# A hybrid attention and SSD layer: sums of squares and split operands made in the SSD stage, output weights asked for throughout the last pair

## The chip, the cores and the metric

The kernel runs on one core of one Trainium2 chip. The metric is the device time of one execution in microseconds. The engines are named as in the profile: PE (TensorE, matmuls), PEld (its weight loads), DVE (VectorE), ACT (ScalarE), POOL (GpSimd) and SP (SyncE, which here only issues DMAs). Sixteen DMA engines serve the core. DMAs are issued from SP's queue or from POOL's.

## The reference, cut to what matters

A decoder layer with two branches. The sequence has 2048 positions, the model 1024 columns. The attention branch has 16 heads in three dilations (1, 4 and 16), combined by their log-sum-exps; the SSD branch is a chunked scan over 16 chunks of 128 positions. Each branch is gated, normed by its root mean square, and multiplied with its half of the output weights.

```python
y_att = rms_norm(y_att.reshape(Bsz, S, D_ATT) * jax.nn.silu(z_att), att_norm_g[layer])
...
y = ssd_chunked(xs_h, dt, a, bm, cm)
y = y + d_skip[layer].astype(jnp.float32)[:, None] * xs_h
y_ssm = rms_norm(y.reshape(Bsz, S, D_SSM).astype(x.dtype) * jax.nn.silu(z_ssm), ssm_norm_g[layer])

mix = jnp.concatenate([y_att, y_ssm], axis=-1)
out = jnp.einsum('bse,ed->bsd', mix, w_out[layer])
x = layer_norm(alpha * x + out, ln_g[layer], ln_b[layer])
```

with `rms_norm(u, g) = u * rsqrt(mean(u * u) + 1e-5) * g`. The gain g is folded into the output weights, so the kernel multiplies the gated rows as they are and scales each product by the row's own rsqrt afterwards. For that it needs two things of every gated block: its split into a high and a low part for the matmuls, and the sum of its squares along the columns.

## The kernel before, in words

All large matmuls are made in three parts: each operand x is split into hi (x rounded to the matmul's format) and lo = x - hi, and hi*hi, hi*lo and lo*hi are accumulated.

The first half of the kernel works through input projections (`proj`, 24 matmuls for each block of 512 positions, lines 104 to 114). Its last part is the SSD stage: while 20 projections of queries, keys and gates run on PE, the 32 units of the scan, `ssd(n, g)` for chunk n and group g, are fed in between (lines 340 to 432), 32 units over 20 projections. A scheduler orders the instructions of this half from its own estimates of their durations. A unit ends with `y`, the gated output, 128 columns-in-group by 4 blocks by 128 positions, in fp32 (DVE adds at line 400, POOL multiplies with the gate at line 401). Line 402 stores y to the DRAM tensor `d_us`. For n under 4 it also splits y into yh (ACT) and yl (DVE) and stores both to `d_uh` (lines 412 to 418). The tiles of yh and yl are those of the unit's `xdeh` and `xdel`, one buffer each.

The second half is the attention, in eight pairs of heads, each with three dilations d, four quarters qd and two halves: 24 steps a pair. Order on PE, DVE, ACT and POOL is written out by hand (`manual_schedule`); only SP's queue is ordered by the scheduler. A step issues `scores` for itself, `transposes` for the step two before and `values` for the step three before; `at` in the loop is the (d, qd, half) of the `values` step. ACT copies finished numerators into tiles `num`. After a pair, its statistics go out to DRAM (`statistics`, d_st), come back in another layout (`gather`, cm), become weights (`weights`), go out (d_wd) and come back broadcast over partitions (wb), and `combine(A, d)` multiplies and adds the three dilations. For pairs 0 to 6 that happens during the next pair, on POOL, at four places of its loop (`step`), and the gated result is stored in `d_ua`. For pair 7 nothing of the attention is left to run beside it: `weights` and `combine` of pair 7 stand in the output stage, on DVE, and its result stays in SBUF (`u7`).

The output stage makes 32 products: `product(n, br)` for a block n of 128 positions and a branch br (1 is SSD, 0 is attention), 48 matmuls of 128x128 by 128x512 in two halves of 24, each over the eight row blocks e of the branch's weights, W[8*br + e]. The order is (0,1), (1,1), (2,1), (3,1), then (0,0) to (3,0), then (4,1), (4,0), (5,1), (5,0) and so on. A product (n, 0) needs the result of pair 7; the first four do not. Around it, for each product: `fetch_parts` takes a large tile for the split operand (for br = 1 and n under 4 it is loaded from d_uh), `fetch_raw` loads the unsplit rows (d_us or d_ua), `split` makes hi and lo on ACT and DVE, `squares` squares them on ACT and sums them on DVE into `sr`, and between the halves of the product one small matmul with a column of ones (line 743) sums that over the partitions. `add` takes the root, and adds the scaled product to the residual in `O[n]`; `norm` ends the block.

The output weights `d_wo` are 16 loads of 1 MB (`load_w`) into tiles that the attention has used: 8 to 15 (SSD) during pair 7 into old key, query, v and permuted-query tiles, 0 to 7 after `combine(A, 2)` in the second turn of the output loop, the first four into `num` tiles. All are issued from POOL's queue, behind whatever POOL has to do.

These lines give the rings that the tiles come from, with their number of buffers:

```python
ring = {"qh": (io, 1), "ql": (io, 1), "qp": (io, 4), "v": (io, 3), "num": (cm_, 6), "wb": (cm_, 3)}
ring.update({f"k{p}_{i}": (qk[i], 1) for p in "hl" for i in range(2)})
```

Of the kernel before, what the change touches and what calls it, by code (L numbers as in the profile page):

```python
# [9 lines left out]
F32 = mybir.dt.float32  # L10
F32R = mybir.dt.float32r
# [17 lines left out]
def hybrid_layer(ctx, tc, xT, xc, w52, wv, convw, convb, dtb, alog, dskp, gcol, wout,  # L29
# [26 lines left out]
    d_us = [dtile(f"d_us{g}", [16, 128, 4, 128]) for g in range(2)]  # L56
    d_uh = [dtile(f"d_uh{g}", [4, 128, 2, 4, 128]) for g in range(2)]
# [10 lines left out]
    gc = consts.tile([128, 16], F32, name="gc")  # L68
    def evac(i, o, a):
        if i % 2:  # L70
            nc.vector.tensor_copy(o, a)
        else:
            nc.scalar.copy(o, a)


    with ExitStack() as c1:
# [263 lines left out]
        def ssd(n, g):  # L340
# [61 lines left out]
            nc.sync.dma_start(d_us[g][n], y)  # L402
# [9 lines left out]
            if n < 4:  # L412
                yh, yl = [sd.tile([128, 512], F32R, name=f"xde{p}") for p in "hl"]
                y1 = y.rearrange("p c l -> p (c l)")
                nc.scalar.copy(yh, y1)
                nc.vector.tensor_tensor(yl, y1, yh.bitcast(F32), op=OP.subtract)
                for p, t in enumerate((yh, yl)):
                    nc.sync.dma_start(d_uh[g][n][:, p], v4(t.bitcast(F32)))
# [20 lines left out]
    with ExitStack() as c2:  # L439
# [244 lines left out]
        def fetch_parts(n, br):  # L684

            t = SP[n, br] = free.pop(0) if len(free) else big(UT.pop(0))
            if br and n < 4:
# [3 lines left out]

        def fetch_raw(n, br):
            u = raw[n, br] = row().rearrange("p (c t) -> p c t", t=128)
            if br:
                for g in range(2):
                    (nc.gpsimd if n < 2 else nc.sync).dma_start(u[:, 4 * g:4 * g + 4], d_us[g][n])
            else:
                nc.sync.dma_start(u[:, 0:7], d_ua[n])

        def split(n, br, cs=slice(0, 8)):  # L700

            if br and n < 4:
                return
            u, t = raw[n, br], SP[n, br]
            if not br and cs.stop == 8:
                nc.vector.tensor_copy(u[:, 7, :], u7[n // 4][:, n % 4])
# [3 lines left out]
        def squares(n, br):  # L710
            u = raw.pop((n, br))
            nc.scalar.activation(u, u, AF.Square)
            sr[n, br] = f2(io.tile([128, 2, 256], F32, name="tb1", bufs=1))[:, 0:128]
            nc.vector.tensor_reduce(sr[n, br], u.rearrange("p c t -> p t c"), axis=mybir.AxisListType.X, op=OP.add)  # L714
# [6 lines left out]
        raw, sr = {}, {}  # L721
# [3 lines left out]
        def product(n, br):  # L725
# [4 lines left out]
            for hf in range(2):  # L730
# [10 lines left out]
                if hf == 0:  # L741
                    pn = psN.tile([128, 512], F32, name="N")
                    nc.tensor.matmul(pn[:, 0:1], sr.pop((n, br)), one, start=True, stop=True)  # L743
            free.append(t)
            return pss, pn

        def add(n, br, pss, pn):

            r = small[:, 8 * n + br:8 * n + br + 1]
            nc.scalar.activation(r, pn[:, 0:1], AF.Sqrt, bias=epst, scale=1.0 / D)  # L750
            nc.vector.reciprocal(r, r)
# [28 lines left out]
        def gate(d, eng):  # L780
            num = f2(pairs[7]["num"][d])
            eng.tensor_tensor(num, num, zt7, op=OP.mult)
# [7 lines left out]
        with tc.manual_schedule(engines={E.PE, E.DVE, E.Activation, E.Pool}):  # L790
            for i in range(len(todo) + TA + 1):
# [16 lines left out]
                if i > TA:  # L808
# [10 lines left out]
                    step = ((1, 0, 0), (1, 1, 0), (1, 3, 0), (2, 2, 0))  # L819
                    if pr and at in step:  # L820
# [141 lines left out]
```

## Time and profile before

| | before |
|---|---|
| median of 3 runs | 2193.69 us (2192.73 to 2193.98) |
| the profiled execution's own time | 2193.83 us |
| its span, first to last instruction | 2192.0 us |
| mean granted PE clock | 0.984 |
| PE busy, share of the span | 98% |
| DVE, ACT, POOL busy | 53%, 39%, 38% |
| DMA, mean | 166 GB/s |

Input projections run until about 700 us of the span, the SSD stage from 700 to about 1262, the attention until about 1780, the handover and the output products to the end. A busy PE is not PE at its peak, since matmuls are pipelined; the useful reading is where it is idle, and what ended the idle time. In the timeline and the chain, a row has start, length, engine, line and output<-input. In the waits, a row has the waiting engine and line, the releaser, and after the colon the total, the number of times and the longest, in microseconds.

### The profile page before, as it was taken

Reading aid. Unit: us, or ns where it says so; the run is one execution under the profiler, and the core shown is the slowest. Engines: PE = TensorE matmul, PEld = TensorE weight load, DVE = VectorE, ACT = ScalarE, POOL = GpSimd, SP = SyncE. Lnnn points to the kernel's source line nnn. Section 1 sums busy time; section 2 is a strip of 40 time slices with the busy share of each in tenths; the row PEclk is TensorE's granted clock in tenths of the full one; section 3 lists DMA queues with packets and bytes.
Section 4 is the critical chain, followed back from the end, with each engine's and each line's share of the span. In section 5 each row is a group of like instructions: output and inputs, shape, how many; then the busy total and the mean of one; then the engine's idle time right before and its main releaser. Section 6 shows DMA issues by size and latency. Waiting matters only on the chain.

```text
span 2192.0 us, 37071 instructions
## 1 busy us (share of the span) xinstructions
PE 2138.5 (98%) x13968; PEld 1784.6 (81%) x13968; DVE 1166.2 (53%) x2941; ACT 847.8 (39%) x2289; POOL 838.8 (38%) x589
## 2 busy tenths in 40 slices
PE   8999999999999999999999999999999976999998
PEld 8999888888888888888888878888878865888886
DVE  4000255555223555554544258888888845655655
ACT  4101122223112333232345368887888841222221
POOL 3101010102442455555555321776666670322322
PEclk9999999999999999999999979999999988999999
DMA  8644222224786656555543542777876799232220
GB/s 281 182 133 139 70 78 71 77 71 148 249 262 208 206 194 198 178 190 177 171 157 129 195 148 76 228 219 223 241 216 184 208 360 276 99 104 83 93 84 29
DMA packets 213955, 363.66 MB, mean 166 GB/s; under 512 B 37776, under 2 KB 125968, under 8 KB 203536
## 3 DMA queue, kind: packets, MB, share of 16 engines
q1 hardware_dynamic: 197408, 278.45, 41.8%
q0 software_dynamic: 16368, 82.84, 10.6%
q8 instruction: 110, 1.80, 0.3%
q14 instruction: 69, 0.57, 0.1%
HBM read 226.62 MB, written 134.61 MB: 165 GB/s over the span
## 4 chain that ended last, share of the span: by engine, by line
PE 89%; DMA 4%; DVE 4%; ACT 2%; SPq 1%; issue 1%; POOL 0%; DVEq 0%; POOLq 0%; ACTq 0%
PE pp L112 14%; PE pp L111 14%; PE pp L113 14%; PE N L577 6%; PE T L557 6%; PE S L528 6%; PE S L737 3%; PE S L739 3%; PE S L738 3%; PE pp L155 2%; PE pp L156 2%; PE pp L154 2%; PE T L737 2%; PE T L738 2%; PE T L739 2%; PE ss L386 1%
## 5 line engine op out<-in xcount | busy, mean ns | idle before, releaser
L111 PE MATMUL pp<-xh,whi 128*128 128x512 f32 x1408 | 550.3, 391 | 0.0
L112 PE MATMUL pp<-xl,whi 128*128 128x512 f32 x1408 | 549.6, 390 | 0.0
L113 PE MATMUL pp<-xh,wlo 128*128 128x512 f32 x1408 | 548.5, 390 | 0.0
L544 ACT ACTIVATE P<-P,st 128x256 f32<-128x256 f32 (+1 forms) x768 | 345.4, 452 | 94.7 <-DVE st L536 94.1
L113 PEld LDWEIGHTS pp<-xh,wlo 128*128 128x128 f32 x1408 | 264.3, 188 | 55.4
L111 PEld LDWEIGHTS pp<-xh,whi 128*128 128x128 f32 x1408 | 264.4, 188 | 54.7
L112 PEld LDWEIGHTS pp<-xl,whi 128*128 128x128 f32 x1408 | 264.4, 188 | 54.0
L536 DVE CUSTOM_DVE_ANT_0 P<-S,tb 128x256 f32<-128x256 f32 (+1 forms) x768 | 235.3, 362 | 107.3 <-PE S L528 76.1
L101 POOL TENSOR_TENSOR wlo<-wraw,whi 128x1024 fp32r<-128x1024 f32 x44 | 105.5, 2397 | 365.1 <-ACT whi L100 352.1
L559 DVE COPY PT<-T 128x512 f32<-128x512 f32 (+1 forms) x304 | 196.5, 677 | 2.3 <-PE T L557 2.2
L557 PE MATMUL T<-ident,P 128*128 128x128 f32 x1200 | 179.4, 286 | 6.3 <-DVE PT L559 5.9
L577 PE MATMUL N<-PT,v 128*64 128x128 f32 x2400 | 176.4, 284 | 0.0
L577 PEld LDWEIGHTS N<-PT,v 128*64 128x64 f32 x2400 | 129.2, 138 | 33.2 <-issue 22.6
L557 PEld LDWEIGHTS T<-ident,P 128*128 128x128 f32 x1200 | 129.7, 142 | 31.5 <-DVE PT L559 7.3
L544 ACT ACTIVATION_READ_ACCUMULATOR P<-P,st 128x1 f32 x768 | 144.7, 188 | 0.0
L644 POOL TENSOR_TENSOR wb<-num,wb 128x2048 f32<-128x2048 f32 x21 | 96.3, 4586 | 97.1 <-DMA wb<-d_wd 69.3
L528 PE MATMUL S<-kh,qp 64*128 64x256 f32 (+1 forms) x1024 | 126.3, 306 | 0.0
L379 DVE TENSOR_SCALAR mt<-csb,cs 128x128 f32<-128x128 f32 x256 | 75.2, 363 | 71.2 <-DMA csb<-d_cs 71.2
L714 DVE TENSOR_REDUCE tb<-P 128x128 f32<-128x1024 f32 x32 | 64.0, 2000 | 85.6 <-PE N L743 49.2
L528 PEld LDWEIGHTS S<-kh,qp 64*128 64x128 f32 x1024 | 88.8, 188 | 22.0 <-issue 20.9
L154 PE MATMUL pp<-vh,xh 128*128 128x384 f32 (+1 forms) x304 | 95.0, 320 | 6.0 <-ACT xh L184 5.4
L100 ACT CAST whi<-wraw 128x1024 fp32r<-128x1024 f32 x44 | 46.1, 1047 | 138.3 <-PE pp L112 130.5
(295 smaller groups left out, 3807.1 us busy)
## 6 DMA issues: line engine op xcount, KB each, us to landing
v<-d_v POOLq DMA_DIRECT2D x24, 1024.0 KB, 7.0
wb<-d_wd SPq DMA_DIRECT2D x48, 512.0 KB
wraw<-w SPq DMA_DIRECT2D x44, 512.0 KB
d_wo<-wot SPq DMA_DIRECT2D x32, 512.0 KB
csb<-d_cs SPq DMA_DIRECT2D x32, 512.0 KB
d_v<-vt SPq DMA_DIRECT2D x64, 192.0 KB
d_za<-ev SPq DMA_DIRECT2D x32, 256.0 KB
d_xs<-cvo SPq DMA_DIRECT2D x8, 1024.0 KB
```

The source lines that it names most:

```text
L111: nc.tensor.matmul(ps, hi[:, k, :], h, start=(k == 0), stop=False)
L112: nc.tensor.matmul(ps, hi[:, k, :], l, start=False, stop=False)
L113: nc.tensor.matmul(ps, lo[:, k, :], h, start=False, stop=(k == 7))
L154: nc.tensor.matmul(ps, h, vw[k][0], start=(k == 0), stop=False)
L528: nc.tensor.matmul(ov(sp[h][:, 256 * b:256 * b + w]), A["q"][d][x][hr, blk], kv(A["k"][y][hr]), start=(m == 0), stop=(m == 2))
L536: nc.vector.tensor_tensor_reduce(P[:, h, b, 256 - w:256], sp[h][:, c0:c0 + w], tab[:, h, tab.shape[2] - w:], 1.0, 3.0e38, OP.add, OP.min, ...
L544: nc.scalar.activation(p, p, AF.Exp, bias=stat(A, 0, d, h, blk), scale=-1.0, accum_out=stat(A, 1, d, h, blk))
L557: nc.tensor.transpose(tp[:, h, b], P[:, h, b, 128 * which:128 * which + 128], ident)
L559: nc.vector.tensor_copy(pt[:, :, bl[0]:2], tp[:, :, bl[0]:2])
L577: nc.tensor.matmul(nm[64 * h:64 * h + 64, bq * 128:bq * 128 + 128], v[:, k, 64 * h:64 * h + 64], pts[which][:, h, b], start=(f or not whic ...
L737: nc.tensor.matmul(ps, uh[:, e, :], wh, start=(e == 0), stop=False)
L738: nc.tensor.matmul(ps, uh[:, e, :], wl, start=False, stop=False)
```

## The change

Three parts.

1. In `ssd`, y is no longer stored whole. Every unit now splits y and stores yh and yl in d_uh, which holds all 16 chunks. Every unit also squares y on POOL (into xd), sums over its four blocks on DVE (into cbm), sums over partitions by a matmul with `one` into a new PSUM tile pq, and adds that to column n of a constant tile `ssq` on DVE.
2. In the output stage, SSD operands are loaded finished from d_uh, by POOL's queue. `fetch` stands for `fetch_parts` and `fetch_raw`; `split`, `squares` and the small matmul in `product` are left for br = 0 alone. The roots of all 16 sums are taken at once behind the first product.
3. The requests of the last pair (output weights 8 to 15, pair 7's gate z7, the first two operands) are spread over pair 7 by `last_pair(at)` and one place before it; the first residuals are asked for behind the first product instead of ahead of it.

```diff
@@ ssd @@
             nc.gpsimd.tensor_tensor(y, y, zt, op=OP.mult)
-            nc.sync.dma_start(d_us[g][n], y)
+            nc.gpsimd.tensor_tensor(xd, y, y, op=OP.mult)
+            nc.vector.tensor_reduce(cbm, xd.rearrange("p c l -> p l c"), axis=mybir.AxisListType.X, op=OP.add)
+            pq = ss.tile([128, 512], F32, name="ss")
+            nc.tensor.matmul(pq[:, 0:1], cbm, one, start=True, stop=True)
+            if g:
+                nc.vector.tensor_tensor(ssq[:, n:n + 1], pq[:, 0:1], ssq[:, n:n + 1], op=OP.add)
+            else:
+                nc.vector.tensor_copy(ssq[:, n:n + 1], pq[:, 0:1])
...
-            if n < 4:
-                yh, yl = [sd.tile([128, 512], F32R, name=f"xde{p}") for p in "hl"]
-                ...
+            yh, yl = [sd.tile([128, 512], F32R, name=f"xde{p}") for p in "hl"]
+            y1 = y.rearrange("p c l -> p (c l)")
+            nc.scalar.copy(yh, y1)
+            nc.vector.tensor_tensor(yl, y1, yh.bitcast(F32), op=OP.subtract)
+            for p, t in enumerate((yh, yl)):
+                nc.sync.dma_start(d_uh[g][n][:, p], v4(t.bitcast(F32)))
@@ fetch, product, add @@
+        def fetch(n, br):
             t = SP[n, br] = free.pop(0) if len(free) else big(UT.pop(0))
-            if br and n < 4:
+            if br:
                 for g in range(2):
                     nc.gpsimd.dma_start(t.rearrange("p (a c t) -> p a c t", a=2, t=128)[:, :, 4 * g:4 * g + 4],
                                         d_uh[g][n])
             else:
+                u = raw[n] = row().rearrange("p (c t) -> p c t", t=128)
                 nc.sync.dma_start(u[:, 0:7], d_ua[n])
...
-                if hf == 0:
+                if hf == br == 0:
                     pn = psN.tile([128, 512], F32, name="N")
...
+            r = ssq[:, n:n + 1]
+            if not br:
+                r = small[:, 8 * n:8 * n + 1]
+                nc.scalar.activation(r, pss.pop(1)[:, 0:1], AF.Sqrt, bias=epst, scale=1.0 / D)
+                nc.vector.reciprocal(r, r)
@@ the last pair @@
+        def last_pair(at):
+            if at == (0, 0, 0):
+                load_w(8, "kh_0")
+                load_w(9, "kl_0")
+            elif at == (0, 3, 1):
+                load_w(12, "v")
+            elif at == (1, 0, 0):
+                z7.append(big("num", F32))
+                nc.gpsimd.dma_start(z7[0], d_za[7])
+            elif at == (1, 1, 0):
+                fetch(0, 1)
+            elif at == (1, 3, 0):
+                load_w(13, "qp")
+                load_w(14, "qp")
+                gate(0, nc.gpsimd)
+            elif at == (1, 3, 1):
+                load_w(15, "v")
+                fetch(1, 1)
...
+                    if pr == 7 and at == (0, 3, 0):
+                        load_w(10, "qh")
+                        load_w(11, "ql")
...
-                    elif at == (1, 0, 0):
-                        for e, name in ((8, "kh_0"), (9, "kl_0"), (10, "qh"), (11, "ql"), (12, "v")):
-                            load_w(e, name)
-                    elif at == (1, 1, 0):
-                        zt7 = big("num", F32)
-                        nc.gpsimd.dma_start(zt7, d_za[7])
-                    elif at == (1, 3, 0):
-                        for e, name in ((13, "qp"), (14, "qp")):
-                            load_w(e, name)
-                        fetch_parts(0, 1)
-                        gate(0, nc.gpsimd)
-                    elif at == (1, 3, 1):
-                        load_w(15, "v")
-                    elif at == (2, 2, 0):
-                        fetch_parts(1, 1)
@@ output stage @@
-            fetch_raw(0, 1)
-            squares(0, 1)
-            residual(0)
-            fetch_raw(1, 1)
-            residual(1)
-            fetch_parts(2, 1)
-            fetch_raw(2, 1)
...
                     weights(A, 0)
                     weights(A, 1)
+                    nc.scalar.activation(ssq, ssq, AF.Sqrt, bias=epst, scale=1.0 / D)
+                    nc.vector.reciprocal(ssq, ssq)
+                    residual(0)
+                    residual(1)
+                    fetch(2, 1)
                     gate(1, nc.vector)
                     gate(2, nc.vector)
                 if i == 1:
-                    fetch_parts(3, 1)
-                    fetch_raw(3, 1)
+                    fetch(3, 1)
...
                 if i == 2:
-                    split(0, 0, slice(0, 7))
+                    split(0, slice(0, 7))
+                if i + 1 < len(order) and not order[i + 1][1]:
+                    split(order[i + 1][0], slice(7, 8) if i == 3 else slice(0, 8))
+                    squares(order[i + 1][0])
+                if 2 <= i < len(order) - 2 and order[i + 2][1]:
+                    residual(order[i + 2][0])
```

The weights 0 to 7, the combine of pair 7 and the order of the 32 products are as they were.

More of the change, by code (lines that the diff above doesn't have):

```diff
@@ L55, in hybrid_layer @@
     d_cs = dtile("d_cs", [256, 128])
-    d_us = [dtile(f"d_us{g}", [16, 128, 4, 128]) for g in range(2)]
-    d_uh = [dtile(f"d_uh{g}", [4, 128, 2, 4, 128]) for g in range(2)]
+    d_uh = [dtile(f"d_uh{g}", [16, 128, 2, 4, 128]) for g in range(2)]
     d_wo = dtile("d_wo", [16, 128, 2, D])
```

57 lines of the change are left out of this document (18 added, 39 removed).

## The prediction

> **What bounds the kernel now.** I read, in this order, the page's busy shares, a table of windows by stage, TensorE's waits, and the chain of waits from the end of the attention onward.
>
> ```profile
> PE 2138.5 (98%) x13968; PEld 1784.6 (81%) x13968; DVE 1166.2 (53%) x2941; ACT 847.8 (39%) x2289; POOL 838.8 (38%) x589
> 700.00:1262.00 562.00, 562.00 (x3043) 462.94 (x3042) 273.61 (x524) 194.84 (x283) 291.11 (x212) 1.00 0.54 181
> 1780.00:1785.00 5.00, 0.00 (x0) 0.00 (x0) 0.00 (x0) 0.34 (x2) 4.98 (x3) 0.77 1.12 385
> 1950.00:2100.00 150.00, 150.00 (x663) 122.12 (x662) 87.16 (x107) 37.81 (x53) 38.16 (x14) 1.00 0.26 85
> PE N L743 <- DVE tb L714: 23.7, 2, 19.2
> PE S L737 <- DMA num<-d_uh: 7.0, 1, 7.0
> ```
>
> A window's columns are its length, then PE, PEld, DVE, ACT, POOL busy, granted clock, DMA share, GB/s. TensorE is the bound: full in the SSD stage (700 to 1262) and in the steady output stage (1950 to 2100), so TensorE work added or removed there counts in full, and other engines' work there counts only if TensorE comes to wait for it (DVE is busy 274 us of 562, POOL 291). The one loss of size is where the attention hands over to the output products: 7.0 us for the first operands, 4.5 and 19.2 us for sums of squares. These are the waits that the change removes; the chain shows what would be late next.
>
> ```profile
> 1777.66 1.92 PE N L577 x32
> ...
> 1781.75 11.66 DMA d_st<-sT
> 1793.49 11.46 DMA cm<-d_st
> ...
> 1807.45 3.21 DMA d_wd<-cm
> ...
> 1814.25 24.14 DMA wb<-d_wd
> 1838.49 2.30 DVE wb L644
> ...
> 1841.42 1.89 DVE PT L649 x3
> ...
> 1865.08 0.39 PE L737 MATMUL S<-num 128*128 128x512 f32 x1
> ```
>
> Columns: start, length, what. Attention ends at 1779.6. Statistics go to DRAM, come back, become weights, go out again and come back broadcast (wb); DVE combines the last pair until 1843.3. Meanwhile TensorE has only the four SSD products (0..3,1); the first attention product, (0,0), which needs the combined pair, starts at 1865.08. The 19.2 us wait is product (2,1) whose sum of squares stands on DVE behind the combine. So 1865 is not the chain's limit: one and a half products were left to do when the chain was through.
>
> **The change, part by part.**
>
> *SSD stage, TensorE.* Each of 32 units gains one matmul of a 128-row column of sums with `one`; the 16 SSD products lose theirs. Its slot is seen in a steady product:
>
> ```profile
> 1995.05 0.39 PE L739 MATMUL S<-wb,num 128*128 128x512 f32 x1
> 1995.28 0.28 PE L743 MATMUL N<-one,tb 128*128 128x1 f32 x2
> ...
> 1995.73 0.39 PE L738 MATMUL S<-num 128*128 128x512 f32 x1
> ```
>
> From 1995.05 to 1995.73 is 0.68 us where two 0.23 steps would be 0.46: 0.22 us each (0.14 if it lands beside other small ones). Added 32 x 0.22 = +7.0 us (4.5 at least), all on the path. Removed where TensorE is full, 12 x 0.22 = -2.6; the other four lie inside the idle stretch.
>
> *SSD stage, other engines.* Per unit POOL gains a square, DVE a reduction and a tiny add, and for the 24 units with n from 4 on ACT a cast, DVE a subtraction. SP issues two d_uh stores in place of one d_us store, or of three for n under 4.
>
> ```profile
> L401 POOL TENSOR_TENSOR y<-y,zt x32: 1284/1289/2220, 706.2 to 1239.6; 128x512 f32<-128x512 f32 x32
> L415 ACT CAST xdeh<-y x8: 621/622/627, 707.5 to 831.8; 128x512 fp32r<-128x512 f32 x8
> L416 DVE TENSOR_TENSOR xdel<-y,xdeh x8: 673/679/683, 710.1 to 834.6; 128x512 fp32r<-128x512 f32 x8
> L714 DVE TENSOR_REDUCE tb<-P 128x128 f32<-128x1024 f32 x32 | 64.0, 2000 | 85.6 <-PE N L743 49.2
>   POOL xdel L371: 11.9, 2
> 1240.91 0.75 POOL L462 DMA_DIRECT2D qh<-d_qh  x1
> 1267.05 0.33 PE L528 MATMUL S<-kh,qh 64*128 64x128 f32 x2
> ```
>
> POOL +32 x 1.29 = 41 us, DVE +32 x 1.15 (half the 2.00 reduction, and 0.15 as an estimate for the add) + 24 x 0.68 = 53, ACT 15: POOL 332 of 562, DVE 327, all beside TensorE; I cost it at nothing. The yh and yl tiles are those of xde, so the next unit waits for the stores; the fifth row is that wait after L418, in units that already stored both halves, and TensorE stayed full. If the cover went, the price is whatever the new matmul waits: 0 to 1.3 us per unit (one POOL square late). The queued work behind a waiting matmul would be projections that need nothing. I take 0, since the stage's many matmuls on DVE, ACT and POOL results cost no idle time now; the upper end is a rival below. The last unit's longer tail delays the first attention loads (from 1240.9 on) by perhaps 5 us; the first scores come at 1267.05, after projections that hide it.
>
> *Last pair.* Weights 8 to 11 are asked for by POOL some 20 us earlier, weight 12 some 12, the gate 10 and the first operands 13. POOL stood idle 16.2 us there, waiting for wb:
>
> ```profile
> 1730.19 1.20 POOL L472 DMA_DIRECT2D v<-d_v  x1
> 1747.60 4.57 POOL L644 TENSOR_TENSOR wb<-num,wb 128x2048 f32<-128x2048 f32 x1 [16.21 <-DMA wb<-d_wd]
> 1764.66 4.60 POOL L644 TENSOR_TENSOR wb<-num,wb 128x2048 f32<-128x2048 f32 x1
> 1765.75 0.57 ACT L587 COPY num<-N 128x512 f32<-128x512 f32 x1
> 1769.04 1.09 PE L557 MATMUL T<-ident,P 128*128 128x128 f32 x8
> ```
>
> The issues fit into it. But v of the third dilation now queues behind four weights (needed only by the third dilation's values), and 6 MB share the engines with wb: the combine starts between 1747.6 and 1755; I take 1750. From there POOL has multiply, gate load, multiply, add, two operand issues, multiply: 4.6+0.6+4.6+4.6+1.4+4.6 = 20.4 us to 1770.4. By program order the operands of (1,1) now take the second old num slot and the third dilation's num takes the slot that this last multiply frees, so ACT's copy at 1765.75 would wait 4.7 us; behind it on ACT stand the exponentials. A step's exponentials are about 3.3 us ahead of their transposes (those that end where the copy starts, 1765.75, feed the transposes of 1769.04), so TensorE loses about 1.5 us; ends 0 and 6.4.
>
> *Handover.* The first operands have landed, so (0,1) starts at once; it may stop for weight 15, which POOL asks for no earlier than before, and that costs nothing because the chain is later. The chain: nothing in it is edited, but it shares DMA engines with less. The raw copies (2 MB here) are gone, the weights mostly moved earlier. Quiet prices from earlier pairs:
>
> ```profile
> 1470.83 1.79 SPq L605 DMA_DIRECT2D d_st<-sT  x4
> 1475.81 0.38 SPq L611 DMA_DIRECT2D cm<-d_st  x1
> 1352.73 0.38 SPq L611 DMA_DIRECT2D cm<-d_st  x1
> 1359.20 0.18 DVE L618 TENSOR_TENSOR mm<-cm 128x32 f32<-128x32 f32 x1
> 1370.00:1375.00 5.00, 5.00 (x64) 4.22 (x62) 4.51 (x20) 3.80 (x16) 0.00 (x0) 1.00 1.04 228
> 1390.00:1395.00 5.00, 5.00 (x60) 4.20 (x60) 4.37 (x17) 3.67 (x14) 4.64 (x5) 1.00 1.12 418
> 1810.68 4.16 SPq L642 DMA_DIRECT2D wb<-d_wd  x6
> ```
>
> Statistics out: 11.2 us now (last issue ends 1782.25), 3.2 quiet; I take 7, as weights 13 to 15, operands and residuals still move then. Back in: 11.5 now, at most 6.5 quiet; I take 8.5. The wb loads: 27.8 us from 1810.68 to 1838.5; 3 MB at the 228 GB/s of a wb stretch is 13.8, 15.5 with latency; I take 21, as weights 0 and 1 and a d_ua row (2.5 MB at 418 GB/s, 6 us) stay beside them. Together 4.2+3.0+6.8 = 14.0 us earlier (ends 0 and 25.3), less the 1.5 of the last pair: combine ends at 1830.8.
>
> What is late next is weights 3 to 7, which POOL issues only behind the slot that the last multiply frees:
>
> ```profile
> 1841.29 0.53 POOL L675 DMA_DIRECT2D num<-d_wo  x1 [7.23 <-issue]
> 1843.61 0.54 POOL L675 DMA_DIRECT2D wb<-d_wo  x1 [0.19 <-issue]
> DMA to landing us min/median/max: 15.0/16.4/17.8
> 1845.00:1850.00 5.00, 4.85 (x12) 3.90 (x13) 4.93 (x8) 0.26 (x1) 0.00 (x0) 0.50 1.03 379
> ```
>
> Weight 7 lands 17.8 us after 1843.61, at 1861.4, 18.1 after the combine. Before, that was hidden by the leftover products; now (0,0) waits for it. I take 16.5 (two d_ua rows can come sooner). Then 0.7 for its last three matmuls, 5.5 for the second half (24 x 0.23), and 2.5 because the clock is at 0.50 after idling (12 matmuls in 5 us): (0,0) ends 25.2 after the combine, at 1856.0, against 1865.1 + 11.3 (48 steps and a sum) = 1876.4 before: -20.4. The Trainium skill, "DMA: Bandwidth & Descriptors", section "Anatomy of one DMA — SWDGE (gpsimd) path", gives 2.0 us plus bytes over 436 GB/s; by that, as an estimate, five weights are there 14 us after the first issue, and the sum would be 2173. The trace's 20 us from 1841.3 to 1861.4, with other transfers alongside, disagrees, and the row is used.
>
> *Steady stage.* Operands of later SSD products come as finished halves through POOL, 1 MB for 0.5 MB at 85 GB/s of traffic, behind the norm's POOL work but two products (22 us) ahead: nothing.
>
> **Sum.** +7.0 - 2.6 - 20.4 = -16.0 on the profiled execution's 2193.83 us (span 2192.0): 2177.8, taken as 2178. The median of the runs is 2193.69, 0.14 lower. Differences under 0.2% (4.4 us) can't be told from no change.
>
> **Rivals.**
> - A, the chain is no faster: saturated engines (share 1.12 at 1780) stay saturated by the weights and residuals. Then (0,0) ends 1843.3+1.5+25.2 = 1870.0, -6.4; total 2191.8. Against: fewer bytes there.
> - B, the chain is quiet: 25.3 us earlier, at 1818; TensorE's four products decide (1779.6 + 4 x 11.3 = 1825, some 7 us later if weight 15 stops the first); (0,0) ends near 1843, -33.5; total 2162.2 with the cheap matmul. Against: 8 MB still to move.
> - C, slower: TensorE runs in order and waits for each new sum of squares, at the end of a chain y, gate, square, reduce over two engines. The cost decides from 16.0/32 = 0.50 us per unit; at one late square of 1.29 it is +41, 2219. For it: L401 took up to 2220 ns in place of 1289, and cbm is now held until the matmul has read it. The Trainium skill, "GPSIMD Engine Reference", section "1. Specifications", says that POOL's memory interfaces are shared with VectorE and contend with its two-input instructions; the 2220 agrees. Against: the full TensorE of 700 to 1262.
> - D, the last pair stalls: combine from 1755, 6.4 us; total 2182.7.
>
> **How the numbers follow.** My case 0.47, A 0.14, B 0.15, C 0.12, D 0.12. Faster: mine, B, D and the better edge of A, 0.77; the same: the rest of A, 0.11; slower: C, 0.12. The range leaves out C and the outermost of B: 2163 to 2196, its top being chain unmoved and D's stall at once (-20.4 vanishes: 2198, trimmed).
>
> **What would show it.** Right: about 32 small matmuls in 700 to 1275 with that stage some 7 us longer and TensorE without idle; no wait of 7 us at the attention's end; one TensorE wait before or inside (0,0), for the combine or for weights 4 to 7; (0,0) ending about 20 us closer to the attention's end. Wrong: TensorE waiting for the reduction in the SSD stage (C), ACT idle at its num copies in the last pair (D), statistics and wb as slow as now (A), or the SSD stage reordered in a way that no row here shows.

## The result, and the profile after

The kernel before took 2193.21 us in the runs beside it (median of 4), the changed kernel 2322.56 us (median of 4): a ratio of 1.0595, 95% interval 1.0577 to 1.0614. The profiled execution of the changed kernel has a span of 2319.6 us against 2192.0. Forecast were 2178 us, and 2163 to 2196 as the range.

The page's busy shares of the changed kernel, then a table of windows (length, then PE, PEld, DVE, ACT, POOL busy, granted clock, DMA share, GB/s):

```profile
PE 2170.9 (94%) x14000; PEld 1810.5 (78%) x14000; DVE 1160.6 (50%) x2986; ACT 835.8 (36%) x2272; POOL 868.6 (37%) x641
```

```profile
700.00:1240.00 540.00, 540.00 (x2811) 446.37 (x2811) 248.25 (x474) 185.72 (x266) 237.81 (x178) 1.00 0.47 160
1240.00:1399.00 159.00, 61.51 (x323) 50.62 (x321) 68.78 (x140) 30.70 (x47) 68.42 (x63) 0.58 0.31 106
```

TensorE is as full in the first 540 us of the SSD stage as it was before. Then it is busy for 61.5 of 159 us, at a clock of 0.58. No other engine is near full there. The list of TensorE's waits from 1240 to 1400 says what it waits for (total, times, longest):

```profile
PE ss L406 <- DVE cbm L404: 69.6, 9, 8.6
PE ss L386 <- DVE mt L382: 21.8, 8, 3.9
PE S L535 <- DMA kh<-d_kh: 6.5, 1, 6.5
```

L406 is the new matmul of the sums (in the kernel before, the number is that of the state matmul, which is L414 in the changed kernel). It waits nine times, in the last nine units. Until then it never waits, but its place shows. Here is the timeline of TensorE in the stretch where projections still cover the units, in the kernel before and then in the changed one. Only SSD instructions are shown; what is left out between L396 and L406 of the changed kernel is projections.

```profile
866.01 1.09 PE L386 MATMUL ss<-mt,xdt 128*64 128x128 f32 x16
867.04 1.16 PE L396 MATMUL ss<-bc,H 128*128 128x128 f32 x8
867.95 0.48 PE L406 MATMUL ss<-xdeh,bsh 128*128 128x512 f32 x1
...
868.73 0.60 PE L355 MATMUL ss<-ident,xs 128*128 128x128 f32 x4
```

```profile
872.34 1.09 PE L386 MATMUL ss<-mt,xdt 128*64 128x128 f32 x16
873.36 1.16 PE L396 MATMUL ss<-bc,H 128*128 128x128 f32 x8
...
888.00 0.28 PE L406 MATMUL ss<-one,cbm 128*128 128x1 f32 x2
888.14 0.48 PE L414 MATMUL ss<-xdeh,bsh 128*128 128x512 f32 x1
...
888.92 0.60 PE L355 MATMUL ss<-ident,xs 128*128 128x128 f32 x4
```

Before, a unit's products L386 and L396 are followed at once by its state matmul (xdeh, bsh), and 0.8 us later by the next unit's transposes L355: two units are in flight. After, 13.5 us of projections stand between L396 and the sum, and the state matmul and the next unit's transposes stand behind the sum. Units begin every 23 us in place of every 17, the projections are used up with nine units to go, and these run bare, with nothing else for TensorE to do, one every 18 us:

```profile
1297.38 2.08 PE L396 MATMUL ss<-bc,H 128*128 128x128 f32 x8
1308.04 0.59 PE L406 MATMUL ss<-one,cbm 128*128 128x1 f32 x2 [8.58 <-DVE cbm L404]
...
1309.91 1.06 PE L355 MATMUL ss<-ident,xs 128*128 128x128 f32 x4
```

The table gives three parts of each profiled execution: the start of the first attention score, the attention from there to the end of its last values matmul, and the rest.

| kernel | median us | ratio to before (95%) | first score | attention | rest |
|---|---|---|---|---|---|
| before | 2193.2 | | 1267.1 | 512.7 | 412.2 |
| after | 2322.6 | 1.0577 to 1.0614 | 1399.5 | 531.8 | 388.4 |
| e1_own_targets | 2368.0 | 1.0782 to 1.0818 | 1440.6 | 531.4 | 394.5 |
| e2_deferred_sum | 2270.9 | 1.0345 to 1.0376 | 1344.9 | 529.6 | 394.2 |
| e3_both | 2232.1 | 1.0163 to 1.0197 | 1299.9 | 531.3 | 396.9 |
| e4_no_squares | 2192.3 | 0.9993 to 1.0013 | 1270.0 | 529.5 | 390.1 |
| e5_late_fetch | 2227.3 | 1.0146 to 1.0195 | 1302.9 | 530.8 | 390.2 |
| e6_requests_as_before | 2219.3 | 1.0117 to 1.0150 | 1302.2 | 523.9 | 396.3 |
| e7_square_on_act | 2234.8 | 1.0186 to 1.0226 | 1306.9 | 533.4 | 390.9 |
| e8_first_four_sums | 2199.5 | 1.0024 to 1.0049 | 1276.7 | 528.0 | 393.3 |
| e9_own_slot | 2200.8 | 1.0030 to 1.0060 | 1278.2 | 528.7 | 391.1 |
| e10_old_requests | 2192.3 | 1.0000 to 1.0018 | 1276.7 | 516.0 | 396.4 |
| e11_square_to_xd | 2196.3 | 1.0017 to 1.0037 | 1277.7 | 522.2 | 395.9 |
| e12_own_sum_tile | 2325.6 | 1.0597 to 1.0641 | 1397.8 | 530.8 | 394.0 |
| e13_all_mended | 2203.1 | 1.0045 to 1.0085 | 1277.2 | 523.2 | 400.4 |
| e14_four_sums_spread | 2191.8 | 0.9997 to 1.0018 | 1272.1 | 517.1 | 401.8 |
| e15_four_sums_old | 2184.7 | 0.9965 to 0.9993 | 1269.4 | 515.8 | 395.8 |

The three parts are read from the one profiled execution of each kernel. It lies up to 4.7 us from the median of the kernel's runs, so a sum of parts can miss a difference of medians by a few microseconds.

So the change adds 132.4 us ahead of the attention and 19.1 in it, and takes 23.8 off the rest: 127.7, close to the difference of the spans. Of the 132.4, 97.5 is TensorE idle from 1240 to 1399, some 26 the clock (an estimate: 61.5 us of work at 0.58, times 0.42), and some 7 the new matmuls. Of the 19.1, 6.5 lies in the first pair and 12.1 in the last. The last pair's wait:

```profile
PE T L564 <- ACT P L551: 9.2, 1, 9.2
```

```profile
1899.33 4.59 POOL L651 TENSOR_TENSOR wb<-num,wb 128x2048 f32<-128x2048 f32 x1 [23.08 <-DMA wb<-d_wd]
1904.49 4.58 POOL L651 TENSOR_TENSOR wb<-num,wb 128x2048 f32<-128x2048 f32 x1
1915.12 4.50 POOL L651 TENSOR_TENSOR wb<-num,wb 128x2048 f32<-128x2048 f32 x1
```

```profile
1915.12 4.51 POOL wb L651
...
1919.66 0.58 ACT num L594
1920.24 0.51 ACT P L551 x2
...
1920.79 0.47 PE T L564
```

POOL's three multiplies of pair 6's combine, then the chain of waits: ACT's first copy into the third dilation's num starts 0.03 us after the third multiply ends, and exponentials and transposes stand behind it. The rest is shorter because the chain behind the attention is, at every transfer (start, length, from the chain of waits; then DVE's third multiply of the last combine, from the timeline):

```profile
1933.23 5.43 DMA d_st<-sT
...
1938.81 8.92 DMA cm<-d_st
...
1950.23 2.41 DMA d_wd<-cm
...
1955.74 14.78 DMA wb<-d_wd
...
1980.58 17.64 DMA wb<-d_wo
```

```profile
1975.46 2.29 DVE L651 TENSOR_TENSOR wb<-num,wb 128x2048 f32<-128x2048 f32 x1 [3.65 <-DMA wb<-d_wd]
```

The chain's row for wb ends at 1970.5, where the chain passes to POOL's queue. The last of the wb loads lands later: DVE's third multiply waits for it until 1975.46. The chain's last line is weight 7, of weights 4 to 7, now the last link.

### The profile page after: what moved, and what is told of

Read it like the earlier page. It is cut to its first block, busy times and chain, and to the rows that moved or that the text cites. A ratio compares the mean times of both kernels' runs of the same rounds, so it can differ in the third digit from the quotient of the medians.

```text
span 2319.6 us, 37246 instructions
## 1 busy us (share of the span) xinstructions
PE 2170.9 (94%) x14000; PEld 1810.5 (78%) x14000; DVE 1160.6 (50%) x2986; ACT 835.8 (36%) x2272; POOL 868.6 (37%) x641
## 5 line engine op out<-in xcount | busy, mean ns | idle before, releaser
L564 PEld LDWEIGHTS T<-ident,P 128*128 128x128 f32 x1200 | 131.2, 144 | 40.4 <-ACT P L551 10.7
L155 PE MATMUL pp<-vl,xh 128*128 128x384 f32 (+1 forms) x304 | 96.8, 320 | 0.1
```

What stands on the lines that cost most here:

```text
L155: nc.tensor.matmul(ps, h, vw[k][1], start=False, stop=False)
L564: nc.tensor.transpose(tp[:, h, b], P[:, h, b, 128 * which:128 * which + 128], ident)
```

## The experiments

Times and stages are in the table above. Two causes were suspected in the SSD stage: the place of the sum's PSUM tile in the ring of five (six tiles per unit, granted in the order in which they are written down), and the reuse of xd and cbm as targets.

**Own targets.**

```diff
-nc.gpsimd.tensor_tensor(xd, y, y, op=OP.mult)
-nc.vector.tensor_reduce(cbm, xd...)       # and pq <- cbm
+nc.gpsimd.tensor_tensor(e2, y, y, op=OP.mult)
+nc.vector.tensor_reduce(ones, e2...)      # and pq <- ones
```

> The changed kernel, but the square goes to e2 and the column of sums to the tile of ones (done with by then), so the next unit's xd and cbm wait for neither. The sum's PSUM tile stays where it was, ahead of pst. Theory ring: the ss pool grants its buffers in written order, so pst and the next unit's px can't be placed before the sum's tile is, and that tile waits for y, gate, square and reduction; this is still there, the units still run one after another, some 9 to 11 are left uncovered at about 15 us of idle TensorE each: the SSD stage stays +135 to +170 and the whole 2315 to 2350. Rival targets: the next unit waits for xd and cbm; this is gone, and the whole is 2193 + 7 (32 matmuls at 0.22) + 14 (last pair) - 24 (handover) = 2190. Rival halves: the y halves of all n hold the xde buffers; untouched here, about 2320.

Measured 2368, worse by 45 us than the change. TensorE now waits at the sum eleven times:

```profile
PE ss L406 <- DVE ones L404: 79.3, 11, 7.8
PE ss L386 <- DVE mt L382: 44.3, 10, 5.4
```

That is above the 2315 to 2350 expected by the ring theory, and far from the 2190 of the targets theory. The targets are not the cause where the sum's place in the ring is as in the change. That it got worse is due to e2: e12 below, which differs from this run in the square's tile alone, takes 2325.6. The next unit writes e2 early and xd late.

**The sum in the next unit.** The sum's matmul and its PSUM tile stand behind the next unit's px, ahead of its cbm; targets as in the change.

```diff
+if prev: sumsq(*prev.pop())               # ahead of cbm of the next unit
 cbm = sd.tile([128, 128], F32, name="cbm")
```

> The changed kernel, but the sum's matmul and its PSUM tile stand in the next unit, behind px and ahead of cbm, so no tile of the ring waits for the y chain before px. Square and sum still go to xd and cbm. Theory ring alone: units overlap again, 2190. Theory targets: the next unit's cbm still waits for the sum's matmul, some 5 units are left without projections at 10 to 15 us of idle each: +50 to +75 in the SSD stage, 2235 to 2265. Both at once (each suffices to keep units apart): 2235 to 2265 here and no gain in the run with own targets. Rival halves: about 2320.

Measured 2270.9: a little above the 2235 to 2265 of the two-cause theory. Some 40% of the loss is gone, six units are left bare, and the wait is for cbm's reduction again:

```profile
PE ss L344 <- DVE cbm L418: 40.0, 6, 7.4
```

**Both.** Square to e2, sum to the tile of ones, matmul in the next unit behind pst.

```diff
-(square, reduction, pq, its matmul and add, ahead of pst)
+if prev: sumsq(*prev.pop())               # behind pst: the unit before; pq, matmul, add
+nc.gpsimd.tensor_tensor(e2, y, y, op=OP.mult)      # at the unit's end
+nc.vector.tensor_reduce(ones, e2...)
```

> The changed kernel with both: square to e2, sums to the tile of ones, and the sum's matmul with its PSUM tile in the next unit, behind pst. If ring and targets are the whole cause: SSD stage +7 (32 matmuls at 0.22; at least 4.5), attention +14, handover -24: 2190, between 2185 and 2197. If either alone was the cause, the same. Rival halves (the y halves of all n in the xde buffers, with twice the stores): still above 2250. Rival engines (POOL's square and DVE's reduction overload them): above 2220.

Measured 2232, 42 above what was expected, in the range of the rival engines. Units overlap again, and no unit is bare, but TensorE waits some 16 us in the stage, and the projections from 700 us to the first score take 470 us in place of 462 (from start to next start, idle time left out):

```profile
PE ss L416 <- POOL xdel L381: 5.4, 10, 0.8
PE ss L416 <- ACT xdeh L380: 4.7, 3, 1.7
PE ss L396 <- DVE mt L392: 4.1, 4, 1.8
```

**No squares.**

```diff
-nc.gpsimd.tensor_tensor(xd, y, y, op=OP.mult)   # and reduction, matmul, add
+if not g and not n: nc.vector.memset(ssq, 1024.0)
```

> The changed kernel without the sums of squares: square, reduction, matmul and add are left out and the 16 columns set to a constant, so the output isn't the reference's. The y halves of all n and the last pair's requests stay. Ring or targets: 2183 (the run with both, less 7 of matmuls), SSD stage within 5 us of the kernel before. Rival halves: SSD stage still over 60 us longer, 2250 and up.

This kernel leaves out the sums and sets the columns to a constant. Measured 2192.3, the time of the kernel before and 9 above what was expected. The first score is 3 us late, so the halves for all n and their buffers cost the SSD stage next to nothing: that rival falls. It is the sums that cost 130 us. The rest of the change is no gain either: what the handover wins (22 us) the attention gives back (17).

**The last pair: (1,1) later; the requests put back; the square on ACT.** All three on the run with both.

```diff
 elif at == (1, 3, 1):
     load_w(15, "v")
-    fetch(1, 1)
+elif at == (2, 0, 0):
+    fetch(1, 1)
```

> The run with both mended (e2, ones, deferred sum), and one more edit: the operands of (1,1) are asked for at (2,0,0), behind the third dilation's num tile, in place of (1,3,1), ahead of it. Theory slot: of the six num slots, (1,1) took the one that the second multiply of pair 6's combine freed, so ACT's copy into the third dilation's num waited for the third multiply and the transposes 8 to 9 us behind it. With the order turned round, that copy finds a free slot: the wait at the transposes goes (under 1 us), the last pair is 8 us shorter, and the whole 2232 - 8 = 2224 (2219 to 2228). (1,1)'s operands then land some 10 us later, still ahead of its product. Rival: POOL is late because of the added issues and bytes, whichever tile takes the slot: the wait stays, 2232.

```diff
-at (0,0,0): 8, 9; (0,3,0): 10, 11; (0,3,1): 12; (1,0,0): gate; (1,1,0): (0,1); (1,3,1): (1,1)
+at (1,0,0): 8 to 12; (1,1,0): gate; (1,3,0): (0,1); (2,2,0): (1,1)
```

> The run with both mended, with the last pair's requests put back where the kernel before has them (weights 8 to 12 at (1,0,0), the gate at (1,1,0), weights 13 and 14 and the operands of (0,1) at (1,3,0), those of (1,1) at (2,2,0)). It prices the spread requests. Last pair: the transposes' wait goes, attention some 12 us shorter. Behind the attention: if the shorter tail comes from the raw copies and sums that are gone, it stays near 395 us and the whole is about 2220; if it comes from the requests being earlier, the tail is back near 412 and the whole about 2235. I expect the first for the larger part: 2223.

```diff
-nc.gpsimd.tensor_tensor(e2, y, y, op=OP.mult)
+nc.scalar.activation(e2, y, AF.Square)
```

> The run with both mended, with the square on ACT in place of POOL, everything else the same. In that run TensorE still waited 16 us in the SSD stage, mostly for xdel (POOL), xdeh (ACT) and mt (DVE), and the first score came 33 us later than before. Theory POOL: the square lengthens POOL's part of each unit's cycle; off POOL, the waits fall to a third and the first score comes 12 to 18 us earlier: 2214 to 2221. Rival cycle: the cycle is as long on ACT, or DVE's reduction sets it: 2228 to 2236.

With (1,1) later, the wait stayed:

```profile
PE T L575 <- ACT P L562: 8.0, 1, 8.0
```

So the theory of the slot got no support here. The time, 2227, lies in the range that it forecast, but by luck: the attention is only 0.5 us shorter than in the run with both, and the gain is in the rest (6.7). With the requests back, the wait is gone, and the last pair is 10 us shorter. The attention is shorter by 7 and not by the 12 expected, because the seventh pair takes 4 us longer; TensorE waits 2.2 us there for kl, which was not followed further. The rest is 396.3 us, against 396.9 and 390.2 in the two runs with spread requests: spreading them buys the handover 0 to 6 us and costs the last pair more. With the square on ACT, the time is 2234.8, as the rival has it: POOL's load was not what held the run with both. The Trainium skill, "GPSIMD Engine Reference", section "1. Specifications", has POOL's memory interfaces shared with VectorE; that would favour this edit, and the run shows no gain from it.

**A part of the change alone.** Sums in the SSD stage only for n below 4 (deferred, as in the run with both); n from 4 on as in the kernel before; requests spread, with (1,1) at (2,0,0).

```diff
-nc.sync.dma_start(d_us[g][n], y)
+if n >= 4: nc.sync.dma_start(d_us[g][n], y)
 if n < 4:                                 # halves, and now:
+    (square, reduction; the matmul in the next unit, behind pst)
```

> The kernel before with a part of the change alone: sums of squares made in the SSD stage only for n below 4 (8 of 32 units; e2, ones, deferred sum), whose four products stand at the handover; n from 4 keeps raw copies, splits and sums in the output stage. The last pair's requests are spread, (1,1) behind the third dilation's num. If the cost in the SSD stage goes by units: a quarter of 33, +8 at most and +2 at least; first pair as before, last pair +0 to +3; handover -20: 2193 + 5 + 1 - 20 = 2179, between 2170 and 2190. Rival: the shorter handover needs all raw copies gone: 2190 to 2197.

Measured 2199.5, above the expected 2170 to 2190: the first score is 9.7 us late (at most 8 expected), and the last pair is still 12 us longer than before (at most 3 expected).

**Its slot, its requests.** Of the run just told, once with the third dilation's num tile taken earlier, once with the old requests.

```diff
 elif at == (1, 1, 0):
+    pairs[7]["num"].append(cm_.tile([128, NR, NJ], F32, name="num", bufs=6))
     fetch_parts(0, 1)
```

> The run with sums for the first four alone and spread requests, with one edit: the third dilation's num tile is taken at (1,1,0), ahead of the operands of (0,1), so its slot is one that the first or second multiply of pair 6's combine freed, and (1,1)'s operands take the slot that the third frees. In that run TensorE waited 9.7 us at the transposes, behind ACT's copy into that tile, which began 0.03 us after the third multiply. Theory slot (whichever free slot the third dilation's tile gets decides; asking for (1,1) later did not change which): the wait goes, 2199.5 - 9 = 2190 (2186 to 2193). Rival: POOL's lateness as such: the wait stays, 2199.

```diff
-last_pair(at)                             # e10: spread requests
+(the requests of the last pair as in the kernel before)
```

> The run with sums for the first four alone, with the last pair's requests as in the kernel before. If spreading the requests gives nothing to the handover (tails of 396.3 and 396.9 us with and without it in the runs with all sums) and costs the last pair 12 us: 2199.5 - 12 = 2188 (2184 to 2192), the tail within 4 us of 393. If the spread is what shortens the tail: tail 405 to 412 and the whole 2198 or more.

The first missed: the wait stayed at 9.7 us. The addresses of the num tiles in the built programs say why. The six slots go out in strict rotation, in the order in which tiles are first written, not made: the third dilation's tile is first written at (2,0,1), so an operand asked for at (2,0,0) was still ahead of it in both runs, and it held pair 6's third slot as in the change. So neither this run nor the earlier one with (1,1) at (2,0,0) had tested the theory. The second came at 2192.3, at the upper edge of what was expected: 7 us below the run with spread requests, with a rest only 3 us longer.

**The square back to xd.** The run with all sums deferred and the old requests, with one edit:

```diff
-nc.gpsimd.tensor_tensor(e2, y, y, op=OP.mult)
+nc.gpsimd.tensor_tensor(xd, y, y, op=OP.mult)
```

> The run with all sums deferred and requests as before (2219), with the square written to xd again in place of e2. Its first score came 35 us later than before, of it 16 us of TensorE waiting in the SSD stage. Theory e2: the next unit's exponentials on ACT wait until the reduction has read e2, and that delays mt and the halves; with xd, written late in the next unit, the waits fall to some 6 us: 2207 to 2212. Rival: the waits come from the longer cycle on DVE and POOL whatever the tile, and xd adds one more wait for POOL: 2217 to 2228.

Measured 2196.3, better than expected: the first score comes at 1277.7, 24.5 us earlier. TensorE is full, with all 32 units' sums made in the stage (windows of that run, then its list of waits in the stage):

```profile
700.00:1270.00 570.00, 567.65 (x3097) 467.46 (x3096) 319.47 (x613) 213.72 (x310) 319.12 (x244) 1.00 0.54 180
```

```profile
PE ss L416 <- POOL xdel L381: 1.7, 2, 1.2
PE ss L396 <- DVE mt L392: 0.7, 1, 0.7
```

So what held the runs with all sums deferred was the square in e2, and not POOL or DVE. The waits of the stage (700 to 1270) show it: with the square in e2 (the run with requests as before), ACT's exponential into e2, early in the next unit, stands behind the reduction; with the square in xd, only POOL's late write to xd does, and TensorE does not come to wait for it.

```profile
ACT e L386 <- DVE ones L434: 42.9, 22, 3.8
```

```profile
POOL xd L401 <- DVE ones L434: 113.2, 31, 5.4
```

**The rest of the causes, and a smaller version.**

```diff
-nc.vector.tensor_reduce(cbm, xd...)       # e12: after, with this edit alone; pq <- ones
+nc.vector.tensor_reduce(ones, xd...)
```

> The changed kernel with one edit: the column of sums goes to the tile of ones in place of cbm; the square stays in xd, the sum's matmul and its PSUM tile stay ahead of pst. Theory ring: the place in the ring of five PSUM buffers keeps units apart by itself; the next unit's px still stands behind the sum's matmul, some 9 units stay uncovered, 2322 (2315 to 2330). Rival cbm: the next unit's wait for cbm is what keeps them apart: 2200 to 2275.

```diff
-elif at == (2, 0, 0):                     # e13 (all sums), e14 (n below 4); square in xd
+elif at == (2, 0, 1):
     fetch(1, 1)
```

> The change whole (all sums in the SSD stage, requests spread), with the causes mended: sum to the tile of ones, its matmul and PSUM tile in the next unit, and (1,1)'s operands asked for at (2,0,1), behind the third dilation's first num copy, which so gets the slot freed by the second multiply. Theory slot: the wait at the transposes falls from 8 to 10 us to under 1.5; against the run with requests as before (2196), last pair +1 to +3 and the handover 5 shorter (tails 391 against 396): 2193 (2189 to 2198). Rival, POOL late as such: the wait stays, 2200 to 2206.

> Sums in the SSD stage for n below 4 alone, square in xd, and requests spread with (1,1) at (2,0,1). Against the run with sums for the first four and requests as before (2192): SSD stage 6 shorter (the square in e2 cost the run with all sums 23, a quarter of that here), last pair +1.5, handover 3 to 5 shorter: 2183 (2179 to 2189). Rival, POOL late as such: 2190 to 2196.

> Sums in the SSD stage for n below 4 alone, square in xd, requests as in the kernel before. SSD stage +4 in place of +10, the rest as in the run with the square in e2 (2192): 2186 (2183 to 2190), 0.2 to 0.4% below the kernel before, all of it from a handover some 16 us shorter.

e15 is the run with sums for the first four and the old requests, with the square in xd.

e12 took 2325.6, with nine waits at the sum again: in its written place the sum keeps units apart by itself. Times to the first score: written place and cbm 1399.5 us (the change), written place alone 1397.8 (e12), cbm with the sum in the next unit 1344.9 (e2), neither 1277.7 (e11), before 1267.1. So the written place is enough to leave units bare. For cbm this is less clean: in e2 the sum also still stands ahead of the next unit's pd in the ring, and the record has no run with cbm alone. In e12, e11 and e13 the matmul stands beside its tile. In the built programs the tiles of this ring are first written in the order in which the kernel makes them, without exception in the six versions looked at, so px never comes ahead of the last tile of the unit before it. Whether the tile or the matmul's own wait in TensorE's order holds px up was not tried apart. The number of tiles is not it: e11 takes the same six from the ring of five.

In e13 the third dilation's tile has the slot of the second multiply, and the wait at the transposes is gone. ACT's copy (timeline) waits 2.4 us for that multiply:

```profile
1788.83 0.59 ACT L605 COPY num<-N 128x512 f32<-128x512 f32 x1 [2.37 <-POOL wb L662]
```

The slot theory holds. But the time, 2203, is no better than with the old requests (e11, 2196). Against the run with (1,1) at (2,0,0), the attention is 7.6 us shorter and the rest 10.2 longer. The chain of waits of e13 now leads through POOL and SP:

```profile
1811.65 4.53 POOL wb L677
1816.20 0.38 SPq L678
...
1816.77 9.79 DMA cm<-d_st
```

L677 is the last step of pair 6's combine, L678 its store, and the load of the statistics is queued behind that store on SP. Here that load starts 16.4 us after the attention's end; in e11, with the old requests, 10.1:

```profile
1801.93 7.91 DMA d_st<-sT
1810.00 8.28 DMA cm<-d_st
```

With spread requests POOL starts pair 6's combine 46 to 49 us after the last pair's first score (changed kernel 1850.9 and 1899.3, e13 1731.7 and 1778.2), without them 36 (before 1711.6 and 1747.6, e15 1717.0 and 1752.8), since wb comes later (POOL's wait for it is 23.1 us in the changed kernel, 16.2 before). SP's rows of the last pair, in the kernel before and then in the changed one, show where the time goes:

```profile
1738.39 0.36 SPq L629 DMA_DIRECT2D d_wd<-cm  x1
1740.07 3.69 SPq L642 DMA_DIRECT2D wb<-d_wd  x6
```

```profile
1877.89 0.36 SPq L636 DMA_DIRECT2D d_wd<-cm  x1
1891.09 4.53 SPq L649 DMA_DIRECT2D wb<-d_wd  x6
```

The weights of pair 6 (48 KB) go out 27 us after the pair's first score in both. The loads of wb, which read them back, follow 1.7 us later before and 13.2 in the changed kernel. It is 10.4 to 13.2 us in all twelve kernels with spread requests and 1.7 in the five with the old ones. The requests that the spread puts ahead of this store are output weights 8 to 12: four of them, 4 MB, are issued from 1869.8 to 1871.5, and the DMA share from 1878 to 1891 is 0.98. So the store itself, and not the loads of wb, is late behind the weights. The stall at the slot was one consequence of that lateness, SP's queue the next one.

e15 is the one version that comes out faster, by little: 2184.7 against 2191.1 as medians, ratio of the runs 0.9979 (0.9965 to 0.9993). That is about the 0.2% below which the prediction would not tell a change from none, and the single runs of the two overlap. It makes the sums for n below 4 alone and leaves the requests as they were. In the profiled executions, the first score is 2.3 us later, the attention 3.1 longer and the rest 16.4 shorter. e14, the same with spread requests, is no faster than before, for the same reason as e13: its load of the statistics starts 16.6 us after the attention's end, behind the same store.

## Why the prediction was wrong, step by step

- **Other engines in the SSD stage, "I cost it at nothing": the step that failed.** The durations were right or on the safe side (square 1.29 forecast, 1.04 measured; reduction 1.0 and 1.08), and so was the full TensorE of the covered stretch. The mistake was to take TensorE's order of instructions as given and to ask only what each would wait for. With the sum's tile and matmul written at the end of the y chain, the state matmul and the next unit's first matmuls stood behind that chain. Units began every 23 us in place of 17, nine were left bare, and the first score came 132 us late. The last sign of being wrong that the prediction names, a stage reordered in a way that no row shows, is what came; it had no price and no chance.
- **Rival C** had the right chain (y, gate, square, reduction) and named cbm, but as waits of TensorE in the covered stage, 0.50 us per unit to decide and 2219 in all. In the covered stage TensorE waited for nothing; the price was paid by nine units with no projections left to cover them, and by the clock. "The queued work behind a waiting matmul would be projections that need nothing" was so, and it was what hid the loss.
- **SSD matmuls, +7.0: of the right size.** Where the units overlap (e11), the new matmuls take 4.4 us from start to next start, just under the least of 4.5, and the stage is 10.7 longer in all. Of the rest, 2.4 is waits, and the projections take 4.6 longer; no run shows why.
- **"The first scores come after projections that hide it": right for the first score (3 us late without squares), wrong by 5 to 7 us for the pair behind it.** With halves for all n, the first pair takes 75.9 us (74.5 without squares, 76.4 in e11) against 69.4 before; in e15, which stores halves for n below 4 alone, 70.5. TensorE waits there 5.0 us (no squares) and 6.4 us (e11) once for DVE's result st. What makes that late was not followed.
- **Last pair, +1.5, and D.** The mechanism was as forecast: ACT's copy waits for the third multiply. The size was off: I took the combine's start 2.4 us later than before, D 7.4, and it came 12.4 later, so the wait was 9.2 us and the pair 12.1 longer. The price left out was the small store of the pair's weights, held up 13.2 us in place of 1.7 behind the 4 MB asked for ahead of it. That the wait's cure would gain nothing, because SP's queue is next, was not seen.
- **Handover, -20.4, with -2.6 of the steady stage: right, and by the forecast path.** Product (0,0) ends some 75 us after the attention's end in place of 97, 21.4 earlier. The -20.4 contains the 1.5 of the last pair, so 21.9 was forecast for this. The steady stage gives the other 2.4 of the 23.8. The transfers: statistics out 5.4 (7 taken), in 8.9 (8.5), and the wb loads done 22.8 after d_wd had landed (21 taken, 27.8 before). DVE's combine ends 49 us after the attention's end (49.7 forecast), and the last link is weights 4 to 7, as forecast. Of the cause, less was right: with the old requests the rest is still 16 us shorter (e6, e10, e11, e15), so most of it comes from what these four share, which is no raw copies and sums for the first four blocks, and the first residuals asked for later. These were not tried apart. The spread adds 0 to 8 us to that where the stall at the slot is in place, and takes 4 to 6 away where it is mended (e13, e14).
- **The DMA price that was set aside.** The last weight landed 17.6 us after its issue here, against 17.8 in the row of before. The Trainium skill, "DMA: Bandwidth & Descriptors", section "Anatomy of one DMA — SWDGE (gpsimd) path", has 2.0 us plus bytes over 436 GB/s, by which, as an estimate, one such weight takes 4.4 us; the row decides.

## What to carry to other kernels

Before costing a new step in a stage that a scheduler orders, list the tiles that it takes from each ring, when each is granted, and which later tile is granted behind it; a result that comes late should take its tile late, in the next iteration. A full engine does not show that iterations still overlap: count units per us as well, and ask what covers the last ones. When a stall is traced to a slot, look at what made the slot late before curing it: here the lateness only moved to the next queue. And a small store can be held up by large loads asked for just ahead of it, so look at what reads it back.

## What the runs showed that was not expected

- Bare units cost more than their waits: with waits of 8 us between small matmuls the granted clock was 0.58 over 159 us, and four transposes of L355 took 1.06 us in place of 0.60. The Trainium skill, "TensorE: Matmul & The Clock Gate", section "HAM oscillation — how this bites in real kernels", has gaps of over some 3.4 us drop the clock to half; the trace agrees (0.58, with the waits at the sum up to 8.6 us).
- The tile to which a scratch result goes was worth 24 us over 32 units (e6 against e11), at the same instructions: e2, which the next unit writes early, or xd, which it writes late.
- POOL's time for the product of y and the gate has two values. In the kernel before it is 1.28 to 1.29 us in 22 units and 2.20 to 2.22 in ten, and those ten are the ones that run beside DVE's product L382. In the changed kernel none does, and the longest is 1.34. POOL's square, with y as both operands, takes 1.04. The timelines of POOL and of DVE in the kernel before:

```profile
955.10 2.22 POOL L401 TENSOR_TENSOR y<-y,zt 128x512 f32<-128x512 f32 x1
```

```profile
954.94 1.23 DVE L382 TENSOR_TENSOR mt<-mt,cbm 128x1024 f32<-128x1024 f32 x1
```

So the 2220 ns that the prediction read as a sign for rival C goes with DVE working at the same time, and says nothing of a late chain.
